# Value turned through DRAM, the key norm's reciprocal spread, and the up weights on SyncE's queue

## The chip, the cores and the metric

The kernel runs on one core of a Trainium2 chip. The metric is the device time of one execution in microseconds (us). A core has several engines, each with its own instruction stream that it works through in order: TensorE (PE: matmuls, and transposes as matmuls with an identity; PEld: its weight loads), VectorE (DVE), ScalarE (ACT), GpSimd (POOL) and SyncE (SP). SP and ACT also issue DMA transfers, each on a queue of its own. SBUF is the on-chip memory of 128 partitions, PSUM the memory that TensorE writes, DRAM the memory outside.

## The reference

One decoder layer over 512 tokens of width 2048, in float32. After an RMS norm one input product gives all streams; half of the width goes through an RWKV-7 recurrence of 16 heads of 64, the other half through trailing means of 2, 4, 8 and 16 tokens. Both are gated, joined, multiplied by an output matrix and added to the input; a gated embedding and a last norm follow.

```python
z = einsum('btd,dn->btn', rms_norm(x, norm_g), w_in)   # r, k, v, two low-rank inputs, gates, pool
decay = exp(-exp(-softplus(-(w0 + tanh(wd) @ w_up)) - 0.5))
a = sigmoid(a0 + ad @ a_up)
kk = k * k_k                                            # per head of 64
kk = kk / maximum(norm(kk), 1e-12)
k = k * (1 + (a - 1) * k_a)
# per token and head, S is 64 x 64
S = S * w_t + (S @ -kk_t) (kk_t * a_t)^T + v_t k_t^T ;  y_t = S r_t
y = head_group_norm(y) + sum(r * k * r_k) * v
x = x + concat(y * silu(g), pool(u) * pool_scale * silu(gp)) @ w_out
x = x + sigmoid(x @ w_pg + b_pg) * (p @ w_ple)
out = rms_norm(x, final_g)
```

## The kernel before

**Tiling.** Matrices are held transposed, with channels on the 128 partitions and the 512 tokens along the free axis. A float32 product is made of three passes over halves of reduced precision: the streamed weight `raw` is cast to `whi` on ACT (L132) and the rest `wlo` is formed on DVE (L133). The 16 heads are handled as eight pairs j = 0 to 7, a pair filling 128 partitions. A pair's 512 tokens are cut into eight chunks of 64.

**What a pair needs.** The columns r, k, v and g of the input product (`zr`, `zk`, `zv`, `zg` in PSUM, then `sr`, `sk`, `sv`, `sg` in SBUF); the decay and the rate a, made in `decay_and_rate` from two small "up" weights (`ur` and `ar` as loaded, `us`, `as` and `uaz` after their casts, L524 and L525); and the unit key `kk`. The key takes three steps: `prepare_key` squares it, `norm_key` sums the squares per head with a matmul that gives every partition of a head its sum (`pss`), and clamps it (L568), and `scale_key` takes the reciprocal of the whole 128x512 tile on DVE (L572) and multiplies. (What the reference calls the norm's root is folded into the later scaling: the squared norm's reciprocal is used once for the product of two keys.)

**The recurrence by chunks.** `prepare` (L576 on) builds the decayed streams `ar` and `bk` and writes `bk` to DRAM (`bkd`). `scores` multiplies them on TensorE (`pm`, masked into `mt`), writes small triangles of the result to DRAM (`nd`, L651), and loads them back as `n` (L656): 32x32 blocks, the same for four groups of partitions, by an access pattern whose first dimension is a repeat of four. Behind these loads `bg` (L662) brings `bkd` back by blocks of 32. `invert` solves 32x32 triangular systems on DVE in 31 steps of two instructions (`tm` L674, `xw` L678), the result going through DRAM (`xd`) into `x1`. `gather` turns the value `sv` with four TensorE transposes (`pv`) and two ACT copies into `uv` (L707, L708), and finishes the inverse with the products `pq`, `pmv` and `px`, for which DVE first transposes `x1` (`y`, L732). `recur` then walks the eight chunks. Each has a chain of hops: `py` on TensorE, `zs` on DVE (L799), `pu` on TensorE, two copies into `uv` on ACT (L813), `ps` on TensorE, the new state `sbd` on DVE (L825), and again `py`.

**What fills the gaps.** TensorE's next work on other columns stands between the hops: `pump(n)` takes n units off a stream of the input product's passes, which first serves the coming pair's k, r, v and g, and in what is left over the pool's columns. The recurrence takes 6, 9 and 9 units behind its three hops (`HC`). Within the recurrence of pair j the kernel also places work for the next pair: `scores(j + 1)` behind chunk 0, and from hop HS on `HN` = 2 steps of the substitution `invert(j + 1)` per hop.

**What sets the order.** In this stage TensorE's instructions stay in program order (`keep_in_program_order`). For the other engines a scheduler at build time sets the order, by its own costs and by when it reckons data ready, under the program's priorities (`high_priority` for the hops) and its `issue_after` links, which place an instruction behind a named one without making it wait. On the chip each engine then runs its list strictly in order. Weights go through a pool of four raw buffers; all large loads, `nd`, `n`, `bg`, `xd` and `x1` are on SP's queue, the up weights (L354) and the stores of finished columns `yd` (L438, L893) on ACT's.

**What a hop's name means below.** `uv<-pu_2` is the copy of chunk 2; the number behind a name counts instances and carries no meaning.

Of the kernel before, what the change touches and what calls it, by code (L numbers as in the profile page):

```python
# [9 lines left out]
F32 = mybir.dt.float32  # L10
# [5 lines left out]
P = 128  # L16
T = 512
# [17 lines left out]
def trunk_kernel(ctx: ExitStack, tc: tile.TileContext, x, p, norm_g, w_in, mu, w0, w_up, a0, a_up,  # L35
# [312 lines left out]
    def load_ab(j):  # L348
        jc = slice(j * P, (j + 1) * P)
        w2 = []  # L350
        for nm, src in (("u", w_up), ("a", a_up)):
            raw = rw.tile([P, P], F32, name=f"{nm}r{j}", tag=f"l{nm}r")
            for h in range(2):
                nc.scalar.dma_start(out=raw[64 * h:64 * h + 64, :], in_=src[0, :, jc])  # L354
            w2.append((raw, rw.tile([P, P], F32R, name=f"{nm}s{j}", tag=f"l{nm}s")))
        wab[j] = w2

# [47 lines left out]
    def pool_unit(n):  # L405
        g, i = n // 4, n % 2
        win = WINDOWS[g]
        ps = psA.tile([P, T], F32, name=f"zb{n}", tag="acc")
        yield from zcols(ps, f"b{n}")
        if n % 4 < 2:  # L410
            u_ = pp.tile([P, T], F32, name=f"u{n}", tag="u")
            nc.scalar.copy(u_, ps)
            s_ = u_
            w_ = 1
            while w_ < win:
                n_ = pp.tile([P, T], F32, name=f"sw{n}_{w_}", tag="sw")
# [12 lines left out]
        sgp = pp.tile([P, T], F32, name=f"sgp{n}", tag="sgp", bufs=1)  # L429
        silu2(ps, sgp)  # L430
        pq = psM.tile([P, T], F32, name=f"pp{n}", tag="m")
        wh, wl = chunk(f"wp{n}", 0)
        for k in range(2):
            mm3(pq, wh[:, k, :], wl[:, k, :], dh[:, k, :], dl[:, k, :], k == 0, k == 1)
            yield 0
        m = 2 * g + i
        nc.vector.scalar_tensor_tensor(sgp, pq, dp(73, m), sgp, ALU.mult, ALU.mult)
        nc.scalar.dma_start(out=yd[NJ + m], in_=sgp)  # L438

    phl, pn = [], []  # L440

# [70 lines left out]
                assert (nm, j) in zt  # L512
        return zt[nm, j]

    pws, kks, late = {}, {}, [None]

    H1, H2, H3, H4, H5, HE = 6, 12, 20, 8, 13, 40

# [44 lines left out]
    def norm_key(j):  # L563
        kk, kqh, kql = kks[j]
        ps = psM.tile([P, T], F32, name=f"pss{j}", tag="m")
        mm(ps, blk, kqh, start=True, stop=False)
        mm(ps, blk, kql, start=False, stop=True)
        late[0] = nc.vector.tensor_scalar(kk, ps, 1e-24, None, ALU.max)  # L568

    def scale_key(j):  # L570
        k_, kk = need("k", j), kks[j][0]
        nc.vector.reciprocal(kk, kk)  # L572
        nc.vector.scalar_tensor_tensor(kk, k_, pc("k_k", j), kk, ALU.mult, ALU.mult)
        kks[j] = kk


    def prepare(j):
        k_, r_, v_ = need("k", j), need("r", j), need("v", j)
        pw, ipw, tha = pws.pop(j)
        kk = kks.pop(j)  # L580
        if j + 1 < NJ:
            load_ab(j + 1)


        ar = rw.tile([P, NCH // 2, 4, C], F32, name=f"ar{j}", tag="ar", bufs=2)
        bk = rw.tile([P, NCH // 2, 4, C], F32, name=f"bk{j}", tag="bk")
        k4 = kk.rearrange("p (q c t) -> p q c t", c=2, t=C)
        pw4 = pw.rearrange("p (q c) t -> p q c t", c=2)
        i4 = ipw.rearrange("p (q c) t -> p q c t", c=2)
        kp = rw.tile([P, T], F32, name=f"kp{j}", tag="kp")  # L590
        nc.vector.tensor_scalar(kp, tha, dp(33, j), dp(41, j), ALU.mult, ALU.add)
        nc.vector.tensor_tensor(kp, kp, k_, ALU.mult)
        nc.vector.tensor_scalar(tha, tha, 0.5, 0.5, ALU.mult, ALU.add)
        nc.vector.tensor_tensor(ar[:, :, 0::3, :], r_.rearrange("p (q c t) -> p q c t", c=2, t=C),
                                pw4[:, :, :, 1:C + 1], ALU.mult)
        nc.vector.tensor_tensor(bk[:, :, 0::3, :], kp.rearrange("p (q c t) -> p q c t", c=2, t=C), i4, ALU.mult)
        nc.vector.scalar_tensor_tensor(ar[:, :, 1:3, :], k_.rearrange("p (q c t) -> p q c t", c=2, t=C), dp(89, j),
                                       pw4[:, :, :, 0:C], ALU.mult, ALU.mult)
        nc.vector.tensor_tensor(kk, kk, tha, ALU.mult)
        made = nc.vector.tensor_tensor(bk[:, :, 1:3, :], k4, i4, ALU.mult)  # L600
        with tc.issue_after(made.ins):
            nc.vector.scalar_tensor_tensor(kp, r_, dp(49, j), kp, ALU.mult, ALU.mult)
            if gates:
                gates.pop()()
        kph = rw.tile([P, T], F32R, name=f"kph{j}", tag="t", bufs=4)
        kpl = rw.tile([P, T], F32R, name=f"kpl{j}", tag="t", bufs=4)
        split(kph, kpl, kp)

        bkd = dram.tile([P, NCH * P], F32, name=f"bkd{j}", tag="bkd")
        nc.sync.dma_start(out=bkd, in_=bk.rearrange("p q s c -> p (q s c)"))  # L610
        st_[j] = dict(pw=pw, ar=ar, bk=bk, bkd=bkd, v_=v_, kp=(kph, kpl))

    bkn = rw.tile([P, NCH, P], F32, name="bkn")

# [5 lines left out]
    def scores(j):  # L620
# [33 lines left out]
        for i in range(2):  # L654
            t_ = rw.tile([P, 16, 32], F32, name=f"n32{j}_{i}", tag=("kk", "kp")[i])
            n_ = nc.sync.dma_start(out=t_, in_=nd[:, :, :, 16 * i:16 * i + 16, :].rearrange(  # L656
                "a b u r c -> (a b u) r c").unsqueeze(0).to_broadcast([4, 32, 16, 32]))
            nb.append(t_)
        bg = rw.tile([P, NCH, 4, 32], F32, name=f"bg{j}", tag="bk")
        with tc.issue_after(n_.ins):  # L660
            for q in range(4):
                nc.sync.dma_start(out=bg[32 * q:32 * q + 32],  # L662
                                  in_=st_[j]["bkd"].rearrange("(b k) (c q i) -> q k c b i", b=4, q=4, i=32)[q])
        st_[j].update(mt=mt, nb=nb, bv=bv, bg=bg)


    def invert(j):
# [18 lines left out]
        for par in range(2):  # L686
            pb = 64 * (1 - par)
            for b in range(2):
                nc.sync.dma_start(out=x1[pb + 32 * b:pb + 32 * b + 32, :, 32 * b:32 * b + 32],
                                  in_=xd[par, b].rearrange("u i q c -> (i q) u c"))  # L690

        st_[j]["x1"] = x1


    def gather(j):
        d = st_[j]
        v_, mt = d.pop("v_"), d["mt"]
        if j + 1 < NJ:
            prepare_key(j + 1)
            decay_and_rate(j + 1)  # L700

        uv = rw.tile([P, NCH, P], F32, name=f"uv{j}", tag="uv")
        ps = psY.tile([P, T], F32, name=f"pv{j}", tag="y")
        for tt in range(NT):
            tr(ps[:, tt * P:(tt + 1) * P], v_[:, tt * P:(tt + 1) * P], ident)
        pv = ps.rearrange("p (t c) -> p t c", c=P)
        nc.scalar.copy(uv[0:64, 0::2, :], pv[0:64])  # L707
        nc.scalar.copy(uv[64:128, 1::2, :], pv[64:128])  # L708


        if j == 0:
            turn_key(0, 0)
# [1 line left out]
        pump(H4)  # L714

        d.update(uv=uv)
        if j + 1 < NJ:
            norm_key(j + 1)
        pump(H5)
        pump(HX)  # L720

# [9 lines left out]
        with tc.issue_after(late[0].ins):  # L731
            yt = [nc.vector.transpose(y1[pb:pb + 32], x1[pb:pb + 32, :, 0:32]) for pb in (0, 64)]  # L732
        with tc.issue_after(yt[0].ins), tc.issue_after(yt[1].ins):
            end = normed.pop()() if normed else yt[1]
        if j + 1 < NJ:
            with tc.issue_after(yt[0].ins), tc.issue_after(end.ins):
                scale_key(j + 1)
        ps3 = psM.tile([P, 8, 32], F32, name=f"pq2{j}", tag="m")
        units(lambda u, par, pb: mm(ps3[pb + 32:pb + 64, u, :],
# [27 lines left out]
    def recur(j, work, between):  # L767
# [7 lines left out]
        def step():  # L775
            hop[0] += 1
            if hop[0] > HS:
                with tc.issue_after(lead[0].ins):
                    for _ in range(HN):
                        next(work, None)  # L780


# [2 lines left out]
        for ch in range(NCH):  # L785
# [27 lines left out]
                    nc.scalar.copy(uv[pb:pb + 64, ch, hc], psu[hc, hc])  # L813
            step()
            pump(HC2)
            if ch < NCH - 1:
                pss = psS.tile([P, T], F32, name=f"ps{j}_{ch}", tag="s")
                mm(pss[:, 0:P], bkn[:, ch, :], uv[:, ch, :], start=True, stop=True)
# [14 lines left out]
            if ch == NCH - 1:  # L833
                for c0 in range(0, NCH, 4):
# [10 lines left out]
                    for pr in range(2):  # L845
                        yr = slice(64 * pr, 64 * pr + 64)
                        nc.scalar.copy(ysb[yr, c0 // 2:c0 // 2 + 2, :], py4[yr, pr::2, :])
            step()
            if ch == 0:
                between()  # L850
            else:
# [30 lines left out]
        def finish():  # L882
# [7 lines left out]
            def gate_out():  # L890
                nc.vector.tensor_tensor(yo, yo, bv, ALU.add)
                nc.vector.tensor_tensor(yo, yo, sg, ALU.mult)
                nc.scalar.dma_start(out=yd[j], in_=yo)  # L893

            return gate_out

        pending.append(finish)

    HC, HT, HX = (6, 9, 9), 130, 13
    HS, HN = 5, 2  # L900
    HP = 1000
    pending, normed, gates = [], [], []
    need("k", 0)
# [308 lines left out]
```

## Time and profile before

| what | value |
| --- | --- |
| time, median of 3 runs | 1085.23 us (1083.53 to 1088.02) |
| the profiled execution's own time | 1082.7 us |
| its span, first to last instruction | 1081.0 us |
| mean granted TensorE clock | 0.998 of full speed |
| mean DMA rate over the span | 136 GB/s |
| tile `pv` in TensorE's list | 32 transposes, 110.5 to 625.2 us |
| TensorE's longest wait | 6.8 us, at the start (`pt_prm`) |

The stage of the head pairs lies between about 80 us (the first `n` load is at 83.6) and 630 us; then come the output matrix and the embedding's gate. A row of the timeline has the start in us, the duration in us, the engine, line, operation and tiles (out <- in), and in brackets the idle time before it with what ended it. A row of a group has its count after the x, then busy us in all and the mean of one in ns, then the idle time before. A row of a tile has the minimum, median and maximum in ns. The rows that begin "DMA packets" count the packets that started in a window, and of them those under 512 bytes, under 2 KB and under 8 KB, each count including the ones before.

### The profile page before, as it was taken

What the parts mean: (1) busy time and instruction counts of PE and PEld (TensorE: products, weight loads), DVE (VectorE), ACT (ScalarE), POOL (GpSimd) and SP (SyncE); (2) the same over time, 40 slices, a digit from 0 to 9 for tenths busy, and PEclk for the clock granted to TensorE, in tenths of its full rate; (3) what the DMA queues carried; (4) which work ended last, traced back from release to release, by engine and by line L of the source; (5) the groups of instructions that cost most, each with busy time, mean ns of one, the idle gap of its engine ahead of it and who ended that gap; (6) DMA issues with size and microseconds to landing.
All of it is one profiled execution on the core that took longest, in us unless ns stands there. A gap on an engine that the chain in (4) does not pass through costs nothing.

```text
span 1081.0 us, 17106 instructions
## 1 busy us (share of the span) xinstructions
PE 1056.6 (98%) x5996; PEld 872.1 (81%) x5996; DVE 714.0 (66%) x1851; ACT 441.5 (41%) x901; POOL 75.0 (7%) x180
## 2 busy tenths in 40 slices
PE   5999999999999999999999999999999999999996
PEld 4888878888888887878788788888888888888885
DVE  6676978888779789787887857563432424445356
ACT  7633435335335354353352344553222222333337
POOL 2100010110110100200101201000000000000000
PEclk9999999999999999999999999999999999999999
DMA  7434443342634533434435343774434428355434
GB/s 236 117 115 111 139 116 88 116 120 74 168 88 114 144 89 105 120 89 112 106 91 158 100 129 111 239 243 141 171 121 143 166 98 271 122 182 161 169 98 156
DMA packets 212916, 146.94 MB, mean 136 GB/s; under 512 B 68085, under 2 KB 173150, under 8 KB 212830
## 3 DMA queue, kind: packets, MB, share of 16 engines
q1 hardware_dynamic: 192126, 112.28, 35.9%
q10 hardware_dynamic: 20704, 33.56, 9.4%
q8 instruction: 47, 0.77, 0.3%
q14 instruction: 39, 0.32, 0.1%
HBM read 122.21 MB, written 23.07 MB: 134 GB/s over the span
## 4 chain that ended last, share of the span: by engine, by line
PE 91%; DVE 4%; DMA 3%; ACT 2%; issue 1%; ACTq 0%; SPq 0%; DVEq 0%
PE acc_o L157 16%; PE acc_g L157 16%; PE zb L157 14%; PE zv L157 8%; PE zg L157 8%; PE zr L157 8%; PE zk L157 7%; PE py L157 2%; PE pu L157 2%; PE pple L157 2%; PE pm L157 1%; DMA n<-nd 1%; PE pp L157 1%; PE ps L157 1%; DMA xt<-in_x_dram 1%; PE pmv L157 1%
## 5 line engine op out<-in xcount | busy, mean ns | idle before, releaser
L133 DVE TENSOR_TENSOR wlo_g<-raw_g,whi_g 128x512 fp32r<-128x512 f32 x84 | 57.0, 685 | 74.4 <-ACT whi_g L132 72.3
L157 PE MATMUL zb<-hhi,whi_b 128*128 128x512 f32 x256 | 106.0, 414 | 0.0
L133 DVE TENSOR_TENSOR wlo_o<-raw_o,whi_o 128x512 fp32r<-128x512 f32 x64 | 43.9, 690 | 90.9 <-ACT whi_o L132 90.8
L157 PE MATMUL zb<-hhi,wlo_b 128*128 128x512 f32 x256 | 100.4, 392 | 0.0
L157 PE MATMUL acc_o<-whi_o,ylo 128*128 128x512 f32 x256 | 100.2, 391 | 0.0
L157 PE MATMUL acc_o<-whi_o,yhi 128*128 128x512 f32 x256 | 99.9, 390 | 0.0
L157 PE MATMUL zb<-hlo,whi_b 128*128 128x512 f32 x256 | 99.8, 390 | 0.0
L157 PE MATMUL acc_o<-wlo_o,yhi 128*128 128x512 f32 x256 | 99.7, 389 | 0.0
L132 ACT CAST whi_g<-raw_g 128x512 fp32r<-128x512 f32 x84 | 52.0, 621 | 105.3 <-PE acc_g L157 58.9
L157 PE MATMUL acc_g<-whi_g,x2hi 128*128 128x512 f32 x208 | 81.2, 391 | 0.0
L832 POOL TENSOR_SCALAR s0p<-sbd,pw 64x64 f32<-64x64 f32 x96 | 58.0, 604 | 332.0 <-DVE sbd L825 243.5
L157 PE MATMUL acc_g<-wlo_g,x2hi 128*128 128x512 f32 x208 | 80.9, 389 | 0.0
L157 PE MATMUL acc_g<-whi_g,x2lo 128*128 128x512 f32 x208 | 80.6, 389 | 0.0
L132 ACT CAST whi_o<-raw_o 128x512 fp32r<-128x512 f32 x64 | 39.9, 623 | 96.3 <-PE acc_o L157 96.3
L132 ACT CAST whi_b<-raw_b 128x512 fp32r<-128x512 f32 x64 | 39.7, 621 | 86.7 <-PE zb L157 29.2
L133 DVE TENSOR_TENSOR wlo_b<-raw_b,whi_b 128x512 fp32r<-128x512 f32 x64 | 43.6, 683 | 27.3 <-ACT whi_b L132 27.1
L157 PEld LDWEIGHTS zb<-hhi,wlo_b 128*128 128x128 f32 x256 | 48.0, 188 | 10.9
L678 DVE TENSOR_TENSOR xw<-xw,tm 128x60 f32<-128x60 f32 (+24 forms) x248 | 52.1, 210 | 7.0
L157 PEld LDWEIGHTS acc_o<-wlo_o,yhi 128*128 128x128 f32 x256 | 48.1, 188 | 9.9
L157 PEld LDWEIGHTS acc_o<-whi_o,ylo 128*128 128x128 f32 x256 | 48.1, 188 | 9.8
L157 PEld LDWEIGHTS acc_o<-whi_o,yhi 128*128 128x128 f32 x256 | 48.1, 188 | 9.7
L157 PEld LDWEIGHTS zb<-hhi,whi_b 128*128 128x128 f32 x256 | 48.2, 188 | 8.3
(283 smaller groups left out, 2529.6 us busy)
## 6 DMA issues: line engine op xcount, KB each, us to landing
raw_b<-in_w_in_dram SPq DMA_DIRECT2D x64, 256.0 KB
raw_o<-in_w_out_dram SPq DMA_DIRECT2D x64, 256.0 KB
raw_g<-in_w_pg_dram SPq DMA_DIRECT2D x64, 256.0 KB
raw_k<-in_w_in_dram SPq DMA_DIRECT2D x32, 256.0 KB
raw_r<-in_w_in_dram SPq DMA_DIRECT2D x32, 256.0 KB
raw_v<-in_w_in_dram SPq DMA_DIRECT2D x32, 256.0 KB
raw_g<-in_w_in_dram SPq DMA_DIRECT2D x32, 256.0 KB
bkd<-bk SPq DMA_DIRECT2D x8, 512.0 KB
```

The lines of the kernel that those rows point to most:

```text
L132: nc.scalar.copy(hi, raw)
L133: nc.vector.tensor_tensor(lo, raw, hi.bitcast(F32), ALU.subtract)
L157: i = nc.tensor.matmul(*a, **k)
L678: nc.vector.tensor_tensor(xw[:, 0:n_, s + 1:32], xw[:, 0:n_, s + 1:32], tm[:, 0:n_, 0:w_], ALU.add)
L832: nc.gpsimd.tensor_scalar(s0p[hc, :], nxt[hc, hc], pcn[hc], None, ALU.mult)
```

## The change

The change has five parts.

- The value is no longer turned on TensorE. `prepare` writes `sv` to DRAM (`vd`), `scores` loads it back by blocks of 32 (`vg`, four loads behind those of `bg`), and `gather` turns the 32x32 blocks with two DVE transposes straight into `uv`.
- From pair 2 on the key norm is formed in the recurrence before the previous one's end: `prepare_key(j + 2)` in chunk 4 and `norm_key(j + 2)` in chunk 5 of `recur(j)`. ACT copies the sums into `kk`; one row per head goes to DRAM (`nrd`) and comes back as 128 partitions of 8 values (`nr`). In the gather `spread_norm` clamps and inverts these, stores them (`ird`) and loads them back repeated over each head's 64 partitions. `scale_key` then only multiplies. Pairs 0 and 1 stay as they were.
- The substitution starts one hop later (HS 5 to 6), with three steps instead of two at hop 21.
- `load_ab(j + 1)`, the up weights, is issued on SP's queue and moves from `prepare(j)` into `scores(j)`, behind the loads of `n`.
- The stores of `yd` are issued on SP's queue.

```diff
@@ load_ab
-                nc.scalar.dma_start(out=raw[64 * h:64 * h + 64, :], in_=src[0, :, jc])
+                nc.sync.dma_start(out=raw[64 * h:64 * h + 64, :], in_=src[0, :, jc])
@@ pool columns; the same edit in gate_out
-        nc.scalar.dma_start(out=yd[NJ + m], in_=sgp)
+        nc.sync.dma_start(out=yd[NJ + m], in_=sgp)
@@ norm_key
-        late[0] = nc.vector.tensor_scalar(kk, ps, 1e-24, None, ALU.max)
+        if j < 2:
+            late[0] = nc.vector.tensor_scalar(kk, ps, 1e-24, None, ALU.max)
+            return
+        nc.scalar.copy(kk, ps)
+        nrd = dram.tile([2, T], F32, name=f"nrd{j}", tag="nrd")
+        nc.sync.dma_start(out=nrd, in_=kk[0::64, :])
+        nr = rw.tile([P, 8], F32, name=f"nr{j}", tag="nr")
+        nc.sync.dma_start(out=nr, in_=nrd.rearrange("h (p e) -> (h p) e", e=8))
+        nrs[j] = nr
+
+    def spread_norm(j):
+        nr, kk = nrs.pop(j), kks[j][0]
+        nc.vector.tensor_scalar(nr, nr, 1e-24, None, ALU.max)
+        nc.vector.reciprocal(nr, nr)
+        ird = dram.tile([2, T], F32, name=f"ird{j}", tag="ird")
+        nc.sync.dma_start(out=ird.rearrange("h (p e) -> (h p) e", e=8), in_=nr)
+        for h in range(2):
+            nc.sync.dma_start(out=kk[64 * h:64 * h + 64], in_=ird[h:h + 1].to_broadcast([64, T]))
 
     def scale_key(j):
-        nc.vector.reciprocal(kk, kk)
+        if j < 2:
+            nc.vector.reciprocal(kk, kk)
@@ prepare
-        if j + 1 < NJ:
-            load_ab(j + 1)
...
+        vd = dram.tile([P, T], F32, name=f"vd{j}", tag="vd")
+        with tc.issue_after(read[-1].ins) if read else ExitStack():
+            nc.sync.dma_start(out=vd, in_=v_)
@@ scores, behind the loads of n
+        if j + 1 < NJ:
+            with tc.issue_after(n_.ins):
+                load_ab(j + 1)
         bg = rw.tile([P, NCH, 4, 32], F32, name=f"bg{j}", tag="bk")
...
+        vg = st_[j]["vg"]
+        with tc.issue_after(n_.ins):
+            for q in range(4):
+                nc.sync.dma_start(out=vg[32 * q:32 * q + 32],
+                                  in_=st_[j]["vd"].rearrange("(b k) (c q i) -> q k c b i", b=4, q=4, i=32)[q])
@@ gather
-            prepare_key(j + 1)
+            if j == 0:
+                prepare_key(1)
             decay_and_rate(j + 1)
...
-        ps = psY.tile([P, T], F32, name=f"pv{j}", tag="y")
-        for tt in range(NT):
-            tr(ps[:, tt * P:(tt + 1) * P], v_[:, tt * P:(tt + 1) * P], ident)
-        pv = ps.rearrange("p (t c) -> p t c", c=P)
-        nc.scalar.copy(uv[0:64, 0::2, :], pv[0:64])
-        nc.scalar.copy(uv[64:128, 1::2, :], pv[64:128])
+        vg = d.pop("vg")
+        for h in range(2):
+            hr = slice(64 * h, 64 * h + 64)
+            nc.vector.transpose(uv[hr, h::2, :].rearrange("p c (b k) -> p c b k", k=32), vg[hr])
...
-            norm_key(j + 1)
+        if j == 0:
+            norm_key(1)
+        if 0 < j < NJ - 1:
+            with tc.issue_after(read[-1].ins):
+                spread_norm(j + 1)
@@ recur
-                    for _ in range(HN):
+                    for _ in range(HN + (hop[0] == HE1)):
...
+            if j + 2 < NJ and ch == 5:
+                norm_key(j + 2)
...
+            if j + 2 < NJ and ch == 4:
+                prepare_key(j + 2)
...
-    HS, HN = 5, 2
+    HS, HN, HE1 = 6, 2, 21
```

SP's queue in the recurrence of pair 2, from the stores of `nd` on, before:

```order
L651 DMA nd_3698<-mt_3668 32x8x32 x4
L129 DMA raw_r_2_2104<-in_w_in_dram 128x4x128
L656 DMA n_0_3703<-nd_3698 128x1x512
L656 DMA n_1_3705<-nd_3698 128x1x512
L662 DMA bg_3707<-bkd_3565 32x32x32
L129 DMA raw_r_3_2110<-in_w_in_dram 128x4x128
L129 DMA raw_v_0_2147<-in_w_in_dram 128x4x128
```

and of the change:

```order
L671 DMA nd_3717<-mt_3687 32x8x32 x4
L129 DMA raw_r_2_2115<-in_w_in_dram 128x4x128
L676 DMA n_0_3722<-nd_3717 128x1x512
L676 DMA n_1_3724<-nd_3717 128x1x512
L354 DMA ur_3726<-in_w_up_dram 64x128 x2
L129 DMA raw_r_3_2121<-in_w_in_dram 128x4x128
L354 DMA ar_3730<-in_a_up_dram 64x128 x2
L685 DMA bg_3734<-bkd_3583 32x32x32
```

The up weights' loads, which were in ACT's list, now stand between `n` and the first load of `bg`.

ACT's order in the same recurrence, from the copy of chunk 1 to that of chunk 3, before:

```order
L813 COPY uv_3347<-pu_1_3738 64x64 x2
L132 CAST whi_k_3_2035<-raw_k_3_2033 128x512
L373 ACTIVATE sg_3758<-zg_3597 128x512
L132 CAST whi_r_0_2076<-raw_r_0_2074 128x512
L813 COPY uv_3347<-pu_2_3810 64x64 x2
L132 CAST whi_r_1_2082<-raw_r_1_2080 128x512
L132 CAST whi_r_2_2106<-raw_r_2_2104 128x512
L813 COPY uv_3347<-pu_3_3883 64x64 x2
```

and of the change:

```order
L842 COPY uv_3375<-pu_1_3769 64x64 x2
L132 CAST whi_k_3_2040<-raw_k_3_2038 128x512
L373 ACTIVATE sg_3789<-zg_3616 128x512
L525 CAST uaz_570<-ur_3726 64x128
L132 CAST whi_r_0_2081<-raw_r_0_2079 128x512
L524 CAST us_3729<-ur_3726 128x128
L842 COPY uv_3375<-pu_2_3834 64x64 x2
L524 CAST as_3733<-ar_3730 128x128
L525 CAST uaz_571<-ar_3730 64x128
L132 CAST whi_r_1_2087<-raw_r_1_2085 128x512
L132 CAST whi_r_2_2117<-raw_r_2_2115 128x512
L842 COPY uv_3375<-pu_3_3910 64x64 x2
```

Two casts of the up weight `ur` now stand ahead of the copy of chunk 2, and two of `ar` behind it; before, all four came later in the list.

TensorE's order in the gather of pair 3, from the up weights' last product on, before:

```order
L157 MATMUL pa_4308<-ahh,as_3545 128x512
L157 MATMUL pa_4308<-lal,uaz_571 128x512
L161 MATMUL pv_4314<-ident,sv_3355 128x128 x4
L157 MATMUL zb_4229<-hhi,whi_b_0_2224 128x512
L157 MATMUL zb_4229<-hlo,whi_b_0_2224 128x512
```

and of the change:

```order
L157 MATMUL pa_4347<-ahh,as_3733 128x512
L157 MATMUL pa_4347<-lal,uaz_571 128x512
L157 MATMUL zb_4274<-hhi,whi_b_0_2234 128x512
L157 MATMUL zb_4274<-hlo,whi_b_0_2234 128x512
```

The four transposes are gone, and the stream's passes follow at once.

More of the change, by code (lines that the diff above doesn't have):

```diff
@@ L513, in need @@
         return zt[nm, j]
-    pws, kks, late = {}, {}, [None]
+    pws, kks, nrs, read, late = {}, {}, {}, [], [None]
     H1, H2, H3, H4, H5, HE = 6, 12, 20, 8, 13, 40
@@ L607, in prepare @@
         split(kph, kpl, kp)
+        vd = dram.tile([P, T], F32, name=f"vd{j}", tag="vd")
+        with tc.issue_after(read[-1].ins) if read else ExitStack():
+            nc.sync.dma_start(out=vd, in_=v_)
         bkd = dram.tile([P, NCH * P], F32, name=f"bkd{j}", tag="bkd")
         nc.sync.dma_start(out=bkd, in_=bk.rearrange("p q s c -> p (q s c)"))
-        st_[j] = dict(pw=pw, ar=ar, bk=bk, bkd=bkd, v_=v_, kp=(kph, kpl))
+        st_[j] = dict(pw=pw, ar=ar, bk=bk, bkd=bkd, vd=vd, v_=v_, kp=(kph, kpl),
+                      vg=rw.tile([P, NT, 4, 32], F32, name=f"vg{j}", tag="t", bufs=4))
     bkn = rw.tile([P, NCH, P], F32, name="bkn")
@@ L688, in invert @@
             for b in range(2):
-                nc.sync.dma_start(out=x1[pb + 32 * b:pb + 32 * b + 32, :, 32 * b:32 * b + 32],
-                                  in_=xd[par, b].rearrange("u i q c -> (i q) u c"))
+                read.append(nc.sync.dma_start(out=x1[pb + 32 * b:pb + 32 * b + 32, :, 32 * b:32 * b + 32],
+                                              in_=xd[par, b].rearrange("u i q c -> (i q) u c")))
         st_[j]["x1"] = x1
@@ L696, in gather @@
         d = st_[j]
-        v_, mt = d.pop("v_"), d["mt"]
+        mt = d["mt"]
         if j + 1 < NJ:
-            prepare_key(j + 1)
+            if j == 0:
+                prepare_key(1)
             decay_and_rate(j + 1)
         uv = rw.tile([P, NCH, P], F32, name=f"uv{j}", tag="uv")
-        ps = psY.tile([P, T], F32, name=f"pv{j}", tag="y")
-        for tt in range(NT):
-            tr(ps[:, tt * P:(tt + 1) * P], v_[:, tt * P:(tt + 1) * P], ident)
-        pv = ps.rearrange("p (t c) -> p t c", c=P)
-        nc.scalar.copy(uv[0:64, 0::2, :], pv[0:64])
-        nc.scalar.copy(uv[64:128, 1::2, :], pv[64:128])
+        vg = d.pop("vg")
+        for h in range(2):
+            hr = slice(64 * h, 64 * h + 64)
+            nc.vector.transpose(uv[hr, h::2, :].rearrange("p c (b k) -> p c b k", k=32), vg[hr])
         if j == 0:
@@ L716, in gather @@
         d.update(uv=uv)
-        if j + 1 < NJ:
-            norm_key(j + 1)
+        if j == 0:
[3 more added lines that the diff above has]
+                spread_norm(j + 1)
         pump(H5)
@@ L733, in gather @@
         with tc.issue_after(yt[0].ins), tc.issue_after(yt[1].ins):
-            end = normed.pop()() if normed else yt[1]
-        if j + 1 < NJ:
-            with tc.issue_after(yt[0].ins), tc.issue_after(end.ins):
+            if normed:
+                normed.pop()()
+            if j + 1 < NJ:
                 scale_key(j + 1)
@@ L892, in gate_out @@
                 nc.vector.tensor_tensor(yo, yo, sg, ALU.mult)
-                nc.scalar.dma_start(out=yd[j], in_=yo)
+                nc.sync.dma_start(out=yd[j], in_=yo)
             return gate_out
```

## The prediction

> **What bounds the kernel now.** I read the busy times first, then the chain of waits, then what TensorE itself waits for.
>
> ```profile
> PE 1056.6 (98%) x5996; PEld 872.1 (81%) x5996; DVE 714.0 (66%) x1851; ACT 441.5 (41%) x901; POOL 75.0 (7%) x180
> ```
> ```profile
> PE 91%; DVE 4%; DMA 3%; ACT 2%; issue 1%; ACTq 0%; SPq 0%; DVEq 0%
> ```
> ```profile
> PE py L157 <- DVE sbd L825: 1.4, 2, 0.9
> PE px L157 <- issue: 1.1, 1, 1.1
> PE pu L157 <- DVE zs L799: 1.0, 2, 0.6
> PE pbo L157 <- DVE kpl L138: 0.3, 1, 0.3
> ```
>
> TensorE is busy for 98% of the span and carries 91% of the chain. In the stage of the head pairs its order is that of the program, so time goes only if TensorE loses work or waits, and time comes wherever a result that it needs is late. The four rows are all that it waits for between the start and the end of that stage: 1.4 + 1.1 + 1.0 + 0.3 = 3.8 us (numbers in a row: us in total, times, longest). DVE is at 66% and off the path but for these. So relieving DVE can give at most 3.8 us; a new wait, repeated once per head pair, can cost far more. I therefore asked of each moved step: which engine's queue does it stand in now, and what stands behind it?
>
> **The value turn: TensorE loses work.** Around one `pv`:
>
> ```profile
> 327.32 0.39 PE L157 MATMUL pa<-ahh,as 128*128 128x512 f32 x1
> 327.55 0.39 PE L157 MATMUL pa<-lal,uaz 128*128 128x512 f32 x1
> 327.78 0.60 PE L161 MATMUL pv<-ident,sv 128*128 128x128 f32 x4
> 328.14 0.47 PE L157 MATMUL zb<-hhi,whi_b 128*128 128x512 f32 x1
> 328.45 0.39 PE L157 MATMUL zb<-hlo,whi_b 128*128 128x512 f32 x1
> ```
>
> From the start of `pv` to the start of the second `zb` pass 0.67 us; without `pv` it would be one step of the stream, 0.23 us (327.32 to 327.55). So 0.44 us per pair, eight pairs: **3.5 us** off TensorE. The sixteen copies out of PSUM leave ACT, which waits on nothing worth counting here. The new work is one 256 KB store and four loads per pair, and two VectorE transposes in the gather.
>
> **What that and the key norm do to DVE.**
>
> ```profile
> L572 DVE RECIPROCAL kk<-kk 128x512 f32<-128x512 f32 x8 | 26.7, 3338 | 0.0
> L617 DVE STREAM_TRANSPOSE bkn<-bg 128x512 f32<-128x512 f32 x16 | 10.9, 697 | 0.0
> L568 DVE TENSOR_SCALAR kk<-pss 128x512 f32<-128x512 f32 x8 | 5.5, 684 | 0.0
> ```
>
> Six of eight reciprocals leave (3.34 us each) and six clamps (0.68). Two value transposes come in; the nearest row is `bkn<-bg` with 0.70, so 1.4 us per pair. The reciprocal and clamp on 128x8 have no row; by size they are a sixty-fourth of the work, and I take 0.1 to 0.2 us for both. Six pairs net 4.02 - 1.4 - 0.2 = 2.4 us less DVE, but the reciprocal stood after the `y<-x` transposes, and the value transposes stand before them:
>
> ```profile
> 190.64 0.42 DVE L732 STREAM_TRANSPOSE y<-x 32x256 f32<-32x256 f32 x1
> 482.16 0.42 DVE L732 STREAM_TRANSPOSE y<-x 32x256 f32<-32x256 f32 x1
> ```
> ```profile
> 191.84 0.69 PE L157 MATMUL pq<-y,mt 32*32 32x32 f32 x32
> 336.95 0.69 PE L157 MATMUL pq<-y,mt 32*32 32x32 f32 x32
> 483.35 0.69 PE L157 MATMUL pq<-y,mt 32*32 32x32 f32 x32
> ```
>
> The two `y<-x` rows belong to the first and last of the three `pq`, and these are the two tightest gathers: `pq` starts 0.78 and 0.77 us after its second transpose ends. Ahead of it DVE gains 1.4 + 0.2 and loses 0.68, net 0.9 us; and TensorE arrives 0.9 us earlier (0.44 without `pv`, 0.46 since the two `pss` matmuls move to the recurrence). So 1.8 - 0.8 = 1.0 us of wait in each of those two, about half that where the slack is 1.4, and none where it is 2 to 3. Upper end 2.5 us, lower end 0 if the scheduler's new order puts other DVE work behind; I take **+1.2**.
>
> **The relief.** With the long reciprocal gone, `kpl` and `zs` come in time; the `px` wait is an ACT copy queued behind another, and their order changes; starting the substitution a hop later leaves fewer steps ahead of the first `sbd` after the broadcast loads. I take all **3.8 us**; the lower end is 0. Steps of the substitution that move to later hops, three of them at hop 21, are the same instructions. The norm's first store and load are issued in the recurrence before; its reciprocal's store and broadcast loads stand ahead of the filler between the value turn and `pq` (327.78 to 336.95, 9.2 us), and `scale_key` comes after it, without the 3.34 us reciprocal. So they have 12.5 us, and two legs as slow as the first half of `n` (6.2 us from issue to use, rows below) need 12.4. I take nothing; a microsecond late in six pairs would be 6, of which DVE's freed time hides part.
>
> **More packets on SP's queue.** Value loads have the 128-byte runs of `bg`: 65,536 words, 2,048 packets per pair. A stretch in which `bg`'s packets run:
>
> ```profile
> DMA packets 3983, 0.95 MB, mean 184 GB/s; under 512 B 2812, under 2 KB 3983, under 8 KB 3983
> ```
>
> That is 294.85 to 300.00: 3,983 packets in 5.15 us, so 2.6 us for 2,048. Behind them on SP's queue stand the streamed weights, whose pool of four buffers is loaded some three chunks ahead; a chunk is twelve matmuls of 0.23, 2.7 us, and three are 8 us. Hidden; if that lead were used up it would be 2.6 x 7 = 18 us. The `yd` stores are read hundreds of us later.
>
> **The up weights: the term that decides.** They leave ACT's queue, where they were issued a pair ahead, and now stand on SP's queue straight behind the broadcast loads `n`. One recurrence of before, where `n` is issued at a = 284.85:
>
> ```profile
> 284.85 1.20 SPq L656 DMA_DIRECT2D n<-nd  x2
> ```
> ```profile
> 291.05 0.19 DVE L674 TENSOR_TENSOR tm<-i,n 128x31 f32<-128x31 f32 x1 [2.13 <-DMA n<-nd]
> ```
> ```profile
> 290.23 0.42 ACT L813 COPY uv<-pu 64x64 f32<-64x64 f32 x2 [0.48 <-PE pu L157]
> ```
> ```profile
> 292.12 0.38 PE L157 MATMUL ps<-uv,bkn 128*128 128x128 f32 x2
> ```
>
> And the packets of a to a+6, then of each microsecond to a+10:
>
> ```profile
> DMA packets 1481, 0.70 MB, mean 117 GB/s; under 512 B 800, under 2 KB 1315, under 8 KB 1481
> DMA packets 360, 0.26 MB, mean 260 GB/s; under 512 B 0, under 2 KB 311, under 8 KB 360
> DMA packets 191, 0.13 MB, mean 135 GB/s; under 512 B 84, under 2 KB 154, under 8 KB 190
> DMA packets 273, 0.07 MB, mean 74 GB/s; under 512 B 190, under 2 KB 268, under 8 KB 273
> DMA packets 422, 0.22 MB, mean 221 GB/s; under 512 B 6, under 2 KB 421, under 8 KB 421
> ```
>
> `n` is the only transfer there with packets of 2 KB. The last column less the one before it counts them: 166, 49, 36, 5, 0, in all 256, which is all of `n`. It is still running past a+8. Next look at the packets under 512 B. The first quarter of `bg` is 1,024 packets of 128 B, issued at a+1.3; 800 small packets (768, three quarters exactly, and 32 of four bytes that signal ends) are done by a+6, then none for a microsecond, and the last 274 only as `n` ends. So `n` runs on a quarter of the DMA engines, and whatever follows it on SP's queue has a quarter of its rows waiting there until `n` is through. [...]
>
> An up weight's 64 rows, issued next after `n`, thus finish when `n` does. I put their landing at L = a+9.5: `n`'s last packets start after a+8, the up weights' and the signal follow. It is no earlier than a+8.5; and a+10.5 is the late end, since `bg`'s tail, which will stand behind them, has at most six packets left after a+9.
>
> Who waits? The piece of ACT's order in the part on the change: the casts `uaz<-ur` and `us<-ur` now stand between the `uv` copies of chunk 1 and chunk 2, with a weight cast between them. ACT runs in order, so the `uv` copy of chunk 2, which TensorE's `ps` needs, waits for L. The order is alike in the recurrences of pairs 0 to 5, which load for pairs 2 to 7. Their costs:
>
> ```profile
> L524 ACT CAST us<-ur x8: 292/299/300, 39.5 to 473.7; 128x128 fp32r<-128x128 f32 x8
> L525 ACT CAST uaz<-ur x8: 290/298/300, 39.7 to 478.6; 64x128 fp32r<-64x128 f32 x8
> ```
> ```profile
> L132 ACT CAST whi_k<-raw_k 128x512 fp32r<-128x512 f32 x32 | 19.8, 620 | 48.3 <-PE zg L157 27.4 <-issue 5.1 <-DMA ar<-in_a_up_dram 4.0
> ```
> ```profile
> 357.95 1.19 SPq L656 DMA_DIRECT2D n<-nd  x2
> 505.74 1.19 SPq L656 DMA_DIRECT2D n<-nd  x2
> ```
> ```profile
> 366.13 0.38 PE L157 MATMUL ps<-uv,bkn 128*128 128x128 f32 x2
> 512.52 0.38 PE L157 MATMUL ps<-uv,bkn 128*128 128x128 f32 x2
> ```
>
> `ps` can start at L + 0.30 + 0.62 + 0.30 + 0.42 = L + 1.64 = a+11.14. It starts at a+7.27, a+8.18 and a+6.78 in the three shown (the latest and the earliest of the six among them), mean a+7.41. The stall is 3.73 us per recurrence, times six: **+22.4 us**; with the ends of L, 16.4 to 28.4.
>
> **Sum.** -3.5 - 3.8 + 1.2 + 22.4 = +16.3 us on the profiled execution's 1082.7, that is 1099.0. That execution lies 2.5 us under the median of 1085.23, so beside the median **1101.5**, say 1102. With the other ends: 1094 (L early, relief whole, no `pq` wait) to 1113 (L late, no relief, `pq` wait whole).
>
> **Rivals.** *The up weights come in time.* If their rows miss `n`'s engines, nothing is late, and the rest decides: -3.5 - 3.8 + 1.2 = -6.1, 1079. For it: three quarters of `bg` are through by a+6. Against it: exactly one quarter is not, and one late row is enough. It turns at L = a+5.8, where L + 1.64 meets `ps`. 0.14.
>
> *The value turn's price is higher.* Up weights in time, but the new transposes, which write in a finer pattern than `bkn`, take twice 0.70 each: 1.4 us more ahead of `pq` in about four gathers, +5.6, 1085: no change. For it: no row shows this pattern; against: the same size and engine. 0.10.
>
> *The stall also slows the clock.* The windows at the end of the program, with their span, then TensorE's busy time, and the granted clock behind POOL:
>
> ```profile
> 1072.30:1076.60 4.30, 0.00 (x0) 0.00 (x0) 3.45 (x11) 3.88 (x8) 0.00 (x0) 1.00 0.07 27
> 1076.60:1081.00 4.40, 0.00 (x0) 0.00 (x0) 0.00 (x0) 0.00 (x0) 0.00 (x0) 0.50 0.63 227
> ```
>
> After 4.3 us without a matmul the granted clock is 0.50. Stalls of 3.7 lie just under that, the longest above. If each brought the half clock, and it lasted 4.3 us, each would cost 2.15 more: +12.9, 1115. 0.10. [...]
>
> **How the numbers follow.** Forecast 0.66, rivals 0.14, 0.10, 0.10. A measurement of this kernel tells about 0.5%, here 1079.8 to 1090.7, from no change. The likeliest case has its own range of 1094 to 1110; the range down to 1078 and up to 1112 takes in both rivals below and leaves out most of the clock's. Faster 0.12 (most of the first rival); same 0.14 (its rest, and the second); slower 0.74.
>
> **What would show it.** Right: TensorE's waits list `ps` behind an ACT copy, six times, 3 to 5 us each, with ACT idle before `uaz<-ur` until that load lands; no `pv` rows; `kpl`, `zs` and `px` gone from the list. Wrong: `uaz<-ur` starts before a+6, or TensorE's busy time does not fall by about 3.5, or the granted clock shows dips.

## The result: slower by 3.6%, and where the profile puts it

The changed kernel takes 1124.78 us (median of 5 runs, lowest 1123.12) against 1085.23 for the kernel before: a ratio of 1.036, with a 95% interval of 1.0335 to 1.0386. One of the five runs took 5366.6 us, and one run each of two later kernels was slow in the same way; these three stand in the medians but not in the ratios. The forecast was 1102 with a range up to 1112; the sign was right, the size less than half of what came, and the range was missed.

TensorE's waits in the changed kernel, the same view as before (waited for what: us in total, times, longest):

```profile
PE ps L157 <- ACT uv L842: 24.7, 6, 4.7
PE pq L157 <- DVE y L761: 6.1, 4, 4.5
PE acc_o L157 <- ACT whi_o L132: 1.4, 1, 1.4
PE pu L157 <- DVE zs L828: 0.6, 2, 0.4
PE pq L157 <- DVE sw L420: 0.4, 1, 0.4
PE acc_o L157 <- DVE wlo_o L133: 0.3, 1, 0.3
PE py L157 <- DVE sbd L856: 0.2, 1, 0.2
```

The first row is the forecast's mechanism, six times, 24.7 us where 22.4 were forecast. The rows for `px` and `kpl` are gone, those for `zs` and `sbd` are down to 0.6 and 0.2: of the 3.8 us before, 3.0 were won. The second row is far larger than the 1.2 us that were allowed for it, and 4.5 of it is one wait. The two `acc_o` rows lie in the output stage and were not in the kernel before.

The granted clock in the page's 40 slices, and the stretches at half clock (their span, then TensorE's busy time; the clock is the figure behind POOL):

```profile
PEclk9999899999999989999999999999999999999999
```
```profile
124.31:131.14 6.83, 6.83 (x93) 5.89 (x87) 5.11 (x5) 2.92 (x7) 0.40 (x1) 0.50 0.18 63
158.44:161.85 3.41, 3.21 (x9) 2.63 (x10) 2.98 (x10) 1.96 (x5) 1.20 (x2) 0.50 0.51 115
236.95:240.36 3.41, 3.38 (x9) 2.80 (x10) 3.06 (x13) 1.21 (x3) 0.90 (x2) 0.50 0.30 88
315.46:318.87 3.41, 3.41 (x11) 2.67 (x10) 2.31 (x9) 0.87 (x2) 0.88 (x2) 0.50 0.39 103
393.96:400.79 6.83, 5.63 (x15) 4.65 (x16) 4.21 (x15) 3.63 (x9) 0.90 (x2) 0.50 0.40 98
472.47:479.30 6.83, 5.38 (x15) 4.41 (x16) 4.03 (x12) 3.26 (x9) 1.44 (x2) 0.50 0.42 100
sum 30.72, PE 27.83 PEld 23.05 DVE 21.69 ACT 13.84 POOL 5.72; mean PE 4.64 PEld 3.84 DVE 3.61 ACT 2.31 POOL 0.95
```

Six stretches, 30.7 us, go with the long wait in the first gather and with five of the six waits for `uv`; they begin between 1.5 us before and 0.7 us after the wait's end. TensorE is busy for 27.8 us in them at half speed; adding up how much longer each step from one matmul's start to the next took than at full clock gives an estimate of 12.5 us (up to 13.5, depending on the full-clock step that is taken for comparison).

The profiled executions differ by 1123.37 - 1082.7 = 40.7 us. The parts: 24.7 (`ps`) + 12.5 (half clock) + 4.5 (`pq`, first gather) + 2.0 (`pq`, the others) + 1.7 (`acc_o`) - 3.0 (waits gone) - 3.5 (`pv` gone) = 38.9; the rest, 1.8, is not accounted for.

One of the six, to read beside the piece that the prediction shows. SP, ACT and TensorE of the changed kernel:

```profile
303.24 1.19 SPq L676 DMA_DIRECT2D n<-nd  x2
304.47 1.16 SPq L354 DMA_DIRECT2D ur<-in_w_up_dram  x2
```
```profile
304.94 0.60 ACT L373 ACTIVATE sg<-zg 128x512 f32<-128x512 f32 x1
313.61 0.30 ACT L525 CAST uaz<-ur 64x128 fp32r<-64x128 f32 x1 [8.06 <-DMA ur<-in_w_up_dram]
313.81 0.61 ACT L132 CAST whi_r<-raw_r 128x512 fp32r<-128x512 f32 x1
314.33 0.29 ACT L524 CAST us<-ur 128x128 fp32r<-128x128 f32 x1
314.65 0.42 ACT L842 COPY uv<-pu 64x64 f32<-64x64 f32 x2
```
```profile
315.12 0.51 PE L157 MATMUL ps<-uv,bkn 128*128 128x128 f32 x2 [4.41 <-ACT uv L842]
```

ACT stands idle for 8 us in front of a 0.3 us cast while the copy that TensorE needs stands three instructions behind that cast in its list. The load lands at a+10.4 (a = 303.24), where L = a+9.5 was taken, and `ps` starts at a+11.9.

### The profile page after: what moved, and what is told of

It reads as the page before. It is cut to its first block, busy times and chain, and to the rows that moved or that the text cites. A ratio compares the mean times of both kernels' runs of the same rounds, so it can differ in the third digit from the quotient of the medians.

```text
span 1121.6 us, 17166 instructions
## 1 busy us (share of the span) xinstructions
PE 1067.5 (95%) x5964; PEld 879.5 (78%) x5964; DVE 705.4 (63%) x1867; ACT 433.5 (39%) x891; POOL 71.8 (6%) x180
## 5 line engine op out<-in xcount | busy, mean ns | idle before, releaser
L863 POOL TENSOR_SCALAR s0p<-sbd,pw 64x64 f32<-64x64 f32 x96 | 55.6, 579 | 371.4 <-DVE sbd L856 283.2
L132 ACT CAST whi_b<-raw_b 128x512 fp32r<-128x512 f32 x64 | 39.5, 619 | 81.7 <-PE zb L157 31.6
L157 PE MATMUL zk<-hhi,whi_k 128*128 128x512 f32 x128 | 55.8, 436 | 0.0
```

The source lines that it names most:

```text
L132: nc.scalar.copy(hi, raw)
L157: i = nc.tensor.matmul(*a, **k)
L863: nc.gpsimd.tensor_scalar(s0p[hc, :], nxt[hc, hc], pcn[hc], None, ALU.mult)
```

## The experiments

**The up weights: queue, place, engines, or order in ACT's list?** Four kernels, each the changed one with one edit. First, the loads back where they were:

```diff
-                nc.sync.dma_start(out=raw[64 * h:64 * h + 64, :], in_=src[0, :, jc])
+                nc.scalar.dma_start(out=raw[64 * h:64 * h + 64, :], in_=src[0, :, jc])
... and load_ab(j + 1) called in prepare(j) instead of behind n in scores(j)
```

> The changed kernel with one part undone: the up weights are loaded on ACT's queue and in prepare, as before the change. Theory A (the up weights land behind the slow broadcast loads, and ACT's casts of them hold up the copy of chunk 2): the six waits of TensorE for uv (24.7 us) vanish, and with them the half clock that follows five of them (some 10 us), so 1123.4 - 35 = about 1088; the wait of 4.5 us before pq in the first gather stays. Theory B (loads on SP's queue cost because they fill that queue, wherever they stand): the same here, about 1088. Theory C (the loss comes from the value turn, the key norm or the later substitution, and the waits for uv only show it): over 1110.

Measured: 1091.93 us, ratio 1.0047 (1.0025 to 1.0069). No wait for `uv` is left in TensorE's list. That is 33 us less than the changed kernel; theory C falls. The first gather's wait, told below, was already counted in the 1088 expected. What goes with the 4 us above it is more time at half clock in the profiled execution (mean clock 0.990): 10.24 us in the first gather, where the changed kernel had 6.83, 3.41 us in the second gather, and 3.41 us behind a wait of 2.2 us for `whi_o` in the output stage.

Second, the loads stay on SP's queue, and only `load_ab(j + 1)` goes back into `prepare(j)`, so that they are issued ahead of `n`:

> The up weights stay on SP's queue, but are issued in prepare, ahead of the stores of bk, some 10 us before the broadcast loads n. Theory A (place behind n): no wait of TensorE for uv behind chunk 1, about 1088, within 2 us of the kernel with the loads on ACT's queue. Theory B (SP's queue itself): at least half of the 35 us stays, over 1105.

Measured: 1086.39 us, ratio 1.0011 (0.9996 to 1.0026). SP's queue as such costs nothing here: theory B falls, and the place behind `n` decides. By the ratios this is some 4 us better than on ACT's queue, with 10.24 us at half clock in place of 17.07 (mean clock 0.994 and 0.990). The up weight's tile, with what its readers waited for (us, times), in the changed kernel:

```profile
  DMA ur<-in_w_up_dram: 57.1, 8
```

and in this one the list of what ended the idle time before its casts names no DMA at all:

```profile
its engine sat idle before it (us, times) until:
  PE pu L157: 4.4, 3
```

Third, `n` spread out:

```diff
-            n_ = nc.sync.dma_start(out=t_, in_=nd[:, :, :, 16 * i:16 * i + 16, :].rearrange(
-                "a b u r c -> (a b u) r c").unsqueeze(0).to_broadcast([4, 32, 16, 32]))
+            for q in range(4):
+                n_ = nc.sync.dma_start(out=t_[32 * q:32 * q + 32], in_=nd[:, :, :, 16 * i:16 * i + 16, :].rearrange(
+                    "a b u r c -> (a b u) r c"))
```

> The changed kernel with the loads n cut in four each, one for each repeat, of 32 rows; the same bytes, six more issues per pair; the up weights stay behind them on SP's queue. Theory A: n spreads over all engines and ends some 4 us sooner, the up weights land by about 5 us after n's issue, the waits for uv fall from 4 us each to below 1, and the half clock goes: 1086 to 1093. Theory B (SP's queue is too full): it gets six issues more of 0.6 us, so no better than 1123.

Measured: 1095.59 us, ratio 1.0088 (1.0053 to 1.0123). The waits for `uv` are gone although the up weights still follow `n`. Their readers wait as follows:

```profile
  DMA ur<-in_w_up_dram: 3.2, 4
```

So 57.1 us of waiting for the load became 3.2, and in one recurrence the second half landed 2.8 us after its issue (228.75, cast at 231.52), not 9. It is not as clean a proof of the quarter of the engines as hoped: the eight smaller loads were issued between weight loads, over 7 us, so that the up weights were also issued later (7 us after the first `n`), and in ACT's list the casts moved one copy further down. What it does show is that with `n` in this form the same place behind `n` no longer makes the up weights late; whether the spread over the engines, the later issue or the other order does it, was not separated. It stays 9 us slower than the second kernel. Beside the first gather (one wait of 3.4 us before `pq`), its list has waits for the casts of the squared key, whose cause was not tried:

```profile
PE pss L157 <- ACT kqh L137: 4.0, 6, 1.7
PE pss L157 <- DVE kql L138: 2.0, 6, 0.4
```

Fourth, loads as in the change, but the casts held back:

```diff
-            nc.scalar.copy(st, raw)
-            nc.scalar.copy(z_[hi, :], raw[hi, :])
+            with tc.issue_after(tail[-1].ins) if tail else ExitStack():
+                nc.scalar.copy(st, raw)
+                nc.scalar.copy(z_[hi, :], raw[hi, :])
... tail[-1] is the last copy of chunk 3 into uv
```

> The changed kernel with loads as they are, late behind n; only the casts of the up weights are placed behind the copy of chunk 3 in ACT's list. Theory A (the wait comes from the order in ACT's list, the late load alone costs nothing): waits for uv gone, about 1088. If the late load matters in itself (TensorE needs the weights later in the recurrence or the decay is late): part of the waits moves to chunk 4 or to the gather, 1095 to 1115.

Measured: 1089.90 us, ratio 1.0033 (1.0015 to 1.0051). The loads are issued as late as in the changed kernel (1.2 us behind `n` in both), and no wait for `uv` is left. So two things make the wait together, a load that lands at a+10 and a list in which its cast stands ahead of a copy needed at a+7; taking away either one removes it. A part of the 3.5 us above the second kernel is the first gather, whose wait before `pq` is 4.5 us here, as in the changed kernel.

Then the same part alone, put into the kernel before (the queue and the place of `load_ab`, nothing else):

> The kernel before with one part of the change alone: the up weights on SP's queue behind n. Theory A (this part makes the loss): TensorE waits for uv some 4 us in each of six recurrences, 22 to 26 us, and the half clock behind most of these adds 6 to 12: 1085 + 28 to 38, so 1113 to 1123; no wait before pq in the first gather. Theory C (the part costs only together with the others): below 1095.

```profile
PE ps L157 <- ACT uv L814: 23.4, 6, 4.3
```

Measured: 1118.02 us, ratio 1.0299 (1.0279 to 1.0318), clock 0.983. This one part brings 33 of the 39.5 us.

**The half clock: does a wait alone bring it?** The kernel before, with ACT repeating the first copy of chunk 2 in six recurrences; nothing else is added, and the values stay the same:

```diff
-                    nc.scalar.copy(uv[pb:pb + 64, ch, hc], psu[hc, hc])
+                    for _ in range(1 + (N if ch == 2 and j < NJ - 2 and h == 0 else 0)):
+                        nc.scalar.copy(uv[pb:pb + 64, ch, hc], psu[hc, hc])
```

N = 18:

> The kernel before, where ACT repeats the first copy of chunk 2 in six recurrences 18 times (3.8 us more on ACT ahead of ps, of which about 1.5 lie in its slack). Both theories of the clock expect TensorE to wait 2.2 to 2.9 us six times, 13 to 17 us, and the clock to stay at 0.998: 1099 to 1103. If any wait of more than about 2 us halves the clock: over 1106 and a clock below 0.99.

N = 29:

> The same with 29 repeats (6.1 us more on ACT): TensorE waits 4.6 to 5.2 us six times, 28 to 31 us. If a wait longer than about 3.4 us halves the clock for 3.4 us or twice that, as in the changed kernel, it adds another 8 to 13 us, and the granted clock falls to about 0.985: 1120 to 1128. If the half clock of the changed kernel came from something else (the up weights, more DMA), the clock stays at 0.998: 1113 to 1116.

N = 12:

> The kernel before with 12 repeats of the first copy of chunk 2 in six recurrences. By the kernel with 18 repeats, whose waits were 3.5 to 4.2 us, 12 give 2.2 to 2.9 us each, 13 to 17 us in all. If a wait below some 3.4 us leaves the clock alone: clock 0.998 and 1099 to 1102. If shorter waits also halve it: below 0.995 and over 1104.

TensorE's waits for `uv`, for N = 12, 18 and 29 in this order:

```profile
PE ps L157 <- ACT uv L814: 12.6, 6, 2.6
```
```profile
PE ps L157 <- ACT uv L814: 21.1, 6, 4.0
```
```profile
PE ps L157 <- ACT uv L814: 36.7, 6, 6.6
```

| N | waits for `uv` in all, us | time, us | over 1085, less the waits | stretches at half clock behind the waits |
| --- | --- | --- | --- | --- |
| 12 | 12.6 | 1098.78 | 1 | one of 3.41 us |
| 18 | 21.1 | 1112.26 | 6 | five of 3.41 us |
| 29 | 36.7 | 1132.78 | 11 | six of 6.83 us |

The time is the median of two runs each, which for N = 12 lie 3 us apart. The waits came out longer than planned for 18 and 29 (on the mean 3.5 and 6.1 us, at most 4.0 and 6.6), so the numbers expected for both missed; what was asked is answered all the same. With N = 12 one of the six waits brought the half clock, which neither expectation had foreseen. In these three kernels waits alone brought the half clock, with no change of loads: the mean clock of the profiled executions is 0.996, 0.990 and 0.979, against 0.998 before. The surcharge was about 1 us in all, no more than the spread of the runs, at waits of 2.1 us on the mean; 1.2 us per wait that brought it at 3.5; and 1.9 at 6.1.

**The first gather.** In the second kernel above, 2.9 us of wait before `pq` were left in the first gather (the texts below put them at 3.3), and 10.24 us of half clock that begin in the midst of it. In the changed kernel:

```profile
113.76 4.96 SPq L129 DMA_DIRECT2D raw_g<-in_w_in_dram  x2
118.94 0.82 SPq L717 DMA_DIRECT2D x<-xd  x2
```
```profile
123.60 0.22 PE L157 MATMUL pq<-y,mt 32*32 32x32 f32 x2 [4.54 <-DVE y L761]
```

Two weight loads that take 4.96 us to issue stand ahead of `x1` (`x` in the rows) on SP's queue. So the next kernel is the second one, with the loads of `raw_g` in the first gather placed behind those of `x1`:

> The changed kernel with the up weights on SP's queue but issued in prepare, and the first gather's loads of g columns placed behind the loads of x1 on SP's queue. Theory D (in the first gather pq waits because a load of raw_g, whose buffer is not free, stands ahead of x1 on SP's queue): the waits of 1.7 and 1.6 us there and the 3.2 us lost in the half clock around them vanish: 1086.4 - 6 = about 1080. Theory E (pq waits there because DVE has more to do or the value's packets slow the stores of xd): the wait stays, 1086.

Measured: 1087.80 us, ratio 1.0025 (1.0011 to 1.0039). The loads of `x1` were issued 0.8 us earlier than in the second kernel (116.23 for 117.02), and the wait stayed:

```profile
PE pq L160 <- DVE y L763: 4.7, 4, 1.6
```

Theory D falls: DVE works without a pause until `y` in this kernel, so it is not `x1` that `y` waits for. What stands ahead of `y` on DVE, changed kernel, first gather (rows of other lines left out):

```profile
117.03 0.69 DVE L610 TENSOR_TENSOR ar<-sr,pw 128x512 f32<-128x512 f32 x1
...
120.04 0.42 DVE L609 TENSOR_SCALAR tha<-tha 128x512 f32<-128x512 f32 x1
120.37 0.69 DVE L612 TENSOR_TENSOR bk<-kp,ipw 128x512 f32<-128x512 f32 x1
120.97 0.75 DVE L613 SCALAR_TENSOR_TENSOR ar<-sk,dprm,pw 128x512 f32<-128x512 f32 x1
...
122.24 0.74 DVE L370 SCALAR_TENSOR_TENSOR sv<-zv,prm,sv 128x511 f32<-128x511 f32 x1
123.01 0.90 DVE L761 STREAM_TRANSPOSE y<-x 32x256 f32<-32x256 f32 x2
```

The scheduler had put four ops of the next pair's preparation and the shift of `sv` ahead of `y`; in the kernel before, all five stood behind it, and `y` ran at 117.44. In the changed kernel itself the loads of `x1` were issued only from 118.94 on, so there a better order alone could not have brought `y` back to 117.44; how its 4.5 us divide between the two was not separated. The next kernel is the second one with the first pair's value turned on TensorE as before, which takes the value loads off SP's queue there and the two transposes off DVE:

```diff
-        for h in range(2):
+        for h in range(2) if j else ():
             hr = slice(64 * h, 64 * h + 64)
             nc.vector.transpose(uv[hr, h::2, :].rearrange("p c (b k) -> p c b k", k=32), vg[hr])
+        if j == 0:
+            ... the four transposes into pv and the two copies, as before
```

> The changed kernel with the up weights on SP's queue but issued in prepare, and the value of the first pair turned on TensorE as before; pairs 1 to 7 by VectorE. DVE's list then has the y transposes of the first gather ahead of three ops of prepare again. Theory F (in the first gather, the loads vg ahead of xd on SP's queue and the later x1 make the scheduler put prepare's work ahead of y, and pq waits): the waits of 3.3 us in the first gather and the 3.2 us of half clock behind them vanish, against 0.44 for one pv: about 1080.5, faster than before by 4 to 5. If the wait has another cause (the key norm, the later substitution): 1086 or more.

Measured: 1080.73 us, ratio 0.9966 (0.9952 to 0.9979): faster than both kernels. Theory F holds in that the value turn of the first pair makes the wait; whether its loads or its transposes lead the scheduler to the other order was not separated. No half clock is left before the end of the program (mean clock 0.998, as in the kernel before). DVE in the first gather, with `y` right behind the clamp again, then the page's clock row:

```profile
115.61 0.69 DVE L569 TENSOR_SCALAR kk<-pss 128x512 f32<-128x512 f32 x1
116.20 0.89 DVE L769 STREAM_TRANSPOSE y<-x 32x256 f32<-32x256 f32 x2
```
```profile
PEclk9999999999999999999999999999999999999999
```

**The other parts alone, in the kernel before.** The value turn of all pairs:

> The kernel before with the value turn alone (all eight pairs). Theory F: the first gather loses 3 to 6 us (wait and half clock), TensorE is 3.5 us shorter, and in the tightest other gathers pq waits a microsecond more, since DVE keeps the long reciprocal: 1084 to 1090. If the value turn is only a gain: 1081 to 1082.

Measured: 1095.60 us, ratio 1.0094 (1.0071 to 1.0117), worse than any expectation. The mean clock of its executions is 0.994, 0.994, 0.993 and, in the profiled one, 0.943, against 0.998 in the profile before. TensorE waits in the first gather as described, and elsewhere DVE is late again and again. That this is because the value transposes came and the long reciprocal stayed is argued, not shown:

```profile
PE pq L157 <- DVE y L739: 5.6, 3, 3.0
PE py L157 <- DVE sbd L832: 3.2, 5, 1.0
```
```profile
PE pm L157 <- DVE bk L600: 1.9, 2, 1.3
PE pbo L157 <- DVE kpl L138: 1.7, 2, 1.3
```

The key norm's part:

> The kernel before with the key norm's part alone (pairs 2 to 7). If a lighter DVE is worth what TensorE waits for it: the waits for kpl, zs and sbd go (2 to 3 us), and nothing is added: 1081 to 1083. If its four transfers or its place in the recurrence cost: 1085 or more, with waits for pss or kk.

Measured: 1083.02 us, ratio 0.9978 (0.9968 to 0.9989): a gain of 2 us between the medians, with no wait for its transfers. The reason expected for it does not show. The waits for `kpl` and `px` are gone, but those for `sbd` grew from 1.4 to 3.5 us:

```profile
PE py L157 <- DVE sbd L848: 3.5, 4, 1.4
```

The two profiled executions do not differ either (1083.3 and 1082.7 us), so where the 2 us come from stays open. Alone, the value turn loses more than it takes off TensorE; beside the norm and without the first pair, as in the kernel of 1080.73 us, it does not. That the norm pays for it with the DVE time that it frees fits this but was not shown: that kernel has the later substitution and the moved stores and loads as well.

The later substitution and the stores of `yd` on SP's queue were not run alone.

## Why the prediction was wrong in size and right in place

- **What bounds it; value turn, 3.5 us off TensorE.** Right in kind. `pv` is gone, and in the best kernel TensorE is busy for 1053.5 us where it was 1056.6, with seven of eight pairs turned on DVE.
- **Relief, 3.8 us.** 3.0 in the changed kernel. The reason given for it, a lighter DVE, is not enough by itself: with the norm's part alone 4.2 us of such waits are listed. The later substitution, another reason given, was not run alone.
- **The up weights, +22.4 us.** Right: 24.7, six times, at the places named, by the chain named; alone this part costs 33 us with its half clock. L was a+10.4 in the recurrence shown, not a+9.5, at the late end of the range given for it. How the rows of an up weight lie on the DMA engines was inferred from `bg`'s packets, and no run shows it apart. What the trace shows in that recurrence is `n` itself running later than before: of its 256 packets 8 started from a+9 to a+10 (254 packets, 246 of them under 2 KB), where before none did.
- **The clock.** This is the step that failed most. The prediction set the half clock beside the forecast as a rival, 0.10, with the forecast itself at clock 0.998. It is no alternative to the stall but came with it: of the six stalls five brought it, and one more came in the first gather, some 12.5 us in all, which the sum had at nothing. The reading behind it was wrong too. From the last 4.3 us of the program I took it that some four microseconds without a matmul are needed and that stalls of 3.7 lie below. But 4.3 us was only the length of the row. The half clock there begins at 1076.60, right behind a window without a matmul that lasts 3.41 us (from 1073.19; the last section has more such windows), and the run with N = 12 shows a wait of 1.9 us that brought it; with N = 18 five of six did, the longest of them 4.0 us. The price, 2.15 us per stall and +12.9 in all, came close, in part by luck: it was meant for six stalls, and about 3 of the 12.5 us belong to the first gather, which was not among them. It belonged into the sum.
- **The `pq` wait, +1.2 us.** The second step that failed: 6.5 us, 4.5 of it in the first gather. The term set net busy time against slack. It assumed that DVE's list keeps its order but for the ops added and removed. The new list had five other ops ahead of `y` there, and the loads of `x1` came some 4 us later (from 118.94, before from 114.67); both lists could have been read beforehand.
- **More packets on SP's queue, nothing.** For the weights in the head pairs no wait is listed. The 1.4 us wait for `whi_o` in the output stage is new. It stands in every kernel here that has the `yd` stores on SP's queue and the later substitution (0.6 to 2.3 us), and in no other, the value turn alone and the norm alone among them; which of these two it is, or only all parts together, was not tried.
- **Norm's transfers, nothing.** Right: no wait for them is listed, and the norm alone does not lose.
- **The rival "up weights in time", 1079.** That is what the kernel with early loads and the first pair on TensorE comes to, 1080.7. With early loads alone it is 1086.4: the first gather eats the gain.

The sum with the measured terms in the prediction's order: -3.5 - 3.0 + 6.5 + 24.7 + 12.5 = +37.2, against 39.5 between the medians; the 1.7 us of the `acc_o` waits belong to none of its terms.

## What to carry to other kernels

A load moved to another queue has to be asked two things: what is ahead of it there, and where its first reader stands in that engine's list. In this kernel a late load cost nothing until an instruction that waits for it stood ahead of one that the bounding engine needs; then it was enough to issue the load earlier or to move the reader down. In the changed kernel six stalls of 3.95 to 4.72 us went with half clock and one of 3.46 us did not; with N = 12 one of 1.9 us did. Where stalls of this size are forecast on TensorE, the half clock behind them belongs into the same sum, and a change that adds or takes away loads has to be read in every engine's new order, in the first iteration too, before its terms are priced.

## What the runs showed of the hardware

In the changed kernel's profile the six stretches at half clock behind a wait last 3.41 or 6.83 us, and the later five begin 34.13, 112.64, 191.15, 269.65 and 348.16 us after the first, which is 10, 33, 56, 79 and 102 times 3.413 us. So its trace can be read in windows of 3.41 us on that grid. The half clock came also behind a window in which TensorE was not idle throughout. Two neighbouring windows of the kernel with N = 12 (span, TensorE's busy time, and the clock behind POOL):

```profile
524.35:527.76 3.41, 1.53 (x8) 1.16 (x8) 3.13 (x12) 1.78 (x9) 0.32 (x1) 1.00 0.50 138
527.76:531.17 3.41, 3.41 (x11) 2.73 (x10) 1.57 (x6) 0.62 (x1) 0.63 (x2) 0.50 0.90 171
```

A wait of 1.9 us fell wholly into one window, which was then busy for 1.53 of 3.41 us (45%), and the next window ran at half clock. The only wait for `uv` of the changed kernel without that consequence is the sixth, 3.46 us long, which lies astride the border of two windows:

```profile
547.57:550.98 3.41, 1.66 (x8) 1.01 (x6) 0.19 (x1) 0.50 (x2) 0.00 (x0) 1.00 0.37 103
550.98:554.39 3.41, 1.70 (x8) 1.46 (x9) 2.74 (x8) 2.82 (x8) 0.00 (x0) 1.00 0.33 86
554.39:557.81 3.42, 3.42 (x17) 2.62 (x16) 3.12 (x13) 1.03 (x3) 0.91 (x2) 1.00 0.48 111
```

Two windows of 49 and 50% follow each other, and the clock stays at 1.00. With N = 18 a window of 45% stayed without consequence (the first row below):

```profile
224.20:227.61 3.41, 1.52 (x7) 0.91 (x5) 2.41 (x10) 3.01 (x14) 0.00 (x0) 1.00 0.74 193
227.61:231.02 3.41, 2.01 (x10) 1.73 (x11) 1.57 (x7) 1.21 (x6) 0.95 (x2) 1.00 0.81 163
```

In the changed kernel, over the windows of this grid from 18.50 us on, the seven at full clock that were followed by half clock, one of them at the end of the program, had been busy for 0 to 27% (0.91 us at most, from 469.06). The least busy window that was not followed by it had 1.58 of 3.42 us (46%, from 117.48). The two of 45% shown above, with N = 12 and N = 18, went either way. So the busy time of a window alone does not settle it, and what does, these runs do not show.
